# 11 of 16 down batches in seven products, W11 + W12 made in DRAM scratch, and activation forms three steps later, in a two-layer decoder trunk

## The chip, the cores and the metric

The kernel runs on one core of a Trainium2 chip. The metric is the device time of one execution in microseconds (us). The core's engines work side by side: TensorE multiplies, VectorE (DVE), ScalarE (ACT) and GpSimd (POOL) do the element-wise work, and SyncE (SP) issues the large DMAs. Each engine takes its instructions in a fixed order.

## The reference

Two decoder layers over 256 tokens of width 2048, all in float32: a token mixer (attention in layer 0, a gated recurrence in layer 1), then an MLP with a hidden width of 8192, then a gated per-layer embedding. The change is in the MLP; its end touches the embedding's input p.

```python
def sqrelu_mlp(xn, w_up, w_down):
    return jnp.square(jax.nn.relu(xn @ w_up)) @ w_down
...
        h = h + sqrelu_mlp(rmsnorm(h, g_mlp[i]), w_up[i], w_down[i])
        ple_gate = jax.nn.sigmoid(rmsnorm(h, g_ple[i]) @ w_ple_gate[i])
        h = h + ple_gate * (p[i] @ w_ple_proj[i])
```

## The kernel before

**Numbers in two parts.** A float32 operand is split into a high part (a cast, on ACT) and a low part (operand minus high part, on DVE), and a product is the sum of three products of parts. A unit of the weight stream, a *sub*, is 128 x 1024 weights. `stream` (L433) runs over all groups of subs: it has the weights loaded by SP in chunks of two to four subs (`load_to`), splits them three subs ahead of the matmuls (`split_to`, W_SPLIT - 1), and issues the matmuls. Raw chunks lie in a ring of four buffers in the MLP (three `w_raw`, one `big`), split pairs in a ring of six (four `w_hi`/`w_lo`, one pair `v4`, one `big`).

**The MLP.** The hidden width is cut into 16 batches of 512. `up(b)` (L820) makes the transposed hidden values of one batch, 8 subs with matmuls of 512 and 256 columns (L537). Its `evict` (L795) adds two halves (L804, L806), does relu and square on ACT (L807, L808) and splits the result. `down(half, bs)` (L826) multiplies the hidden values of some batches with one half of the columns of `w_down` and adds the product to the residual h. After each pair of up groups stands one down group: the first of batches 0 and 1, then of four batches each ({0..3}, {2..5}, ... {12..15}) with halves alternating, and at the end one more of {14, 15}. Per layer that is six groups of four batches that the change alters, batches up to 3, 5, 7, 9, 11 and 13.

**Seven products.** A down batch is a product of 2 x 2 blocks of the hidden values with 2 x 2 blocks of weights of 128 x 1024: W11 and W21 are the even and odd rows of 128 of the first chunk (512 columns), W12 and W22 those of the second. An even batch (`is_seven`) takes seven products of forms (`FORMS`) in place of eight: 7 subs of 6 matmuls = 42; an odd, plain one 4 subs of 12 = 48. For a seven the hidden side needs sums (L810, L814, L815), and the weight side four sums on DVE (L470): U1 = W11 + W12, T2 = U1 + W22, T3, T4. A form's high part is cast at L464, its low part is made at L471. Plain batches and up groups use L356 and L357. Sums, the evicted halves of a seven and kept products share three buffers of tag `t4`.

**After the products.** `middle` (L832) makes combinations of the products once the last of P1, P5, P6, P7 is there, and `evict` (L843) adds eight parts to h (L848).

**What sets the order.** The code issues a group's work in the order above, with `defer` for work that is to come some subs later; a scheduler then lays each engine's instructions in a row by what they depend on.

## Time and profile before

| | us |
|---|---|
| median of 3 runs | 2304.05 |
| lowest and highest run | 2304.01, 2304.63 |
| the profiled execution | 2303.79 |
| its span from first to last instruction | 2301.9 |
| TensorE busy in it | 2277.8 |
| DVE busy | 1709.6 |
| ACT busy | 1355.5 |

The page gives the busy time of each engine over the whole span. A table by stage gives the same for chosen stretches of time, a list of waits tells which engine waited for which, and a timeline shows single instructions: when one started, how long it took, and how long its engine had been idle before it and for whom. Consecutive instructions of an engine overlap a little, so the distance of their starts is less than their length.

### The profile page before, as it was taken

What the parts mean: (1) busy time and instruction counts of PE and PEld (TensorE: products, weight loads), DVE (VectorE), ACT (ScalarE), POOL (GpSimd) and SP (SyncE); (2) the same over time, 40 slices, a digit from 0 to 9 for tenths busy, and PEclk for the clock granted to TensorE, in tenths of its full rate; (3) what the DMA queues carried; (4) which work ended last, traced back from release to release, by engine and by line L of the source; (5) the groups of instructions that cost most, each with busy time, mean ns of one, the idle gap of its engine ahead of it and who ended that gap; (6) DMA issues with size and microseconds to landing.
All of it is one profiled execution on the core that took longest, in us unless ns stands there. A gap on an engine that the chain in (4) does not pass through costs nothing. (4 is left out here: it accounts for less than half of the span.)

```text
span 2301.9 us, 29004 instructions
## 1 busy us (share of the span) xinstructions
PE 2277.8 (99%) x11275; PEld 1913.4 (83%) x11275; DVE 1709.6 (74%) x2048; ACT 1355.5 (59%) x1836; POOL 47.3 (2%) x79
## 2 busy tenths in 40 slices
PE   8999999999999999999999999999999999999999
PEld 7888888888888888887888887888888888888787
DVE  6676655778878868879666767568887887887974
ACT  6555555655655645646557887555564564564653
POOL 2100000000000000000000000000000000000000
PEclk9999999999999999999999999999999999999999
DMA  7455556456547547545555565645745645745464
GB/s 244 165 185 168 165 171 214 168 182 237 181 162 242 187 161 244 175 162 186 193 190 190 165 201 173 202 157 200 256 151 179 238 167 181 239 167 179 174 210 146
DMA packets 221050, 434.80 MB, mean 189 GB/s; under 512 B 7326, under 2 KB 12064, under 8 KB 220912
## 3 DMA queue, kind: packets, MB, share of 16 engines
q1 hardware_dynamic: 220256, 432.04, 55.5%
q8 instruction: 88, 1.44, 0.3%
q0 software_dynamic: 608, 0.89, 0.2%
q14 instruction: 50, 0.41, 0.1%
q10 hardware_dynamic: 48, 0.02, 0.0%
HBM read 430.82 MB, written 2.10 MB: 188 GB/s over the span
## 5 line engine op out<-in xcount | busy, mean ns | idle before, releaser
L357 DVE TENSOR_TENSOR w_lo<-w_raw,w_hi 128x1024 fp32r<-128x1024 f32 x465 | 564.2, 1221 | 304.5 <-ACT w_hi L356 304.4
L356 ACT CAST w_hi<-w_raw 128x1024 fp32r<-128x1024 f32 x465 | 486.6, 1051 | 419.4 <-PE acc L352 214.9
L537 PE MATMUL acc<-x,w_hi 128*128 128x512 f32 x1368 | 477.3, 396 | 0.0
L350 PE MATMUL acc<-w_hi,x 128*128 128x512 f32 x1152 | 457.1, 397 | 0.0
L351 PE MATMUL acc<-w_lo,x 128*128 128x512 f32 x1152 | 450.4, 391 | 1.9 <-DVE w_lo L357 1.9
L352 PE MATMUL acc<-w_hi,x 128*128 128x512 f32 x1152 | 450.6, 391 | 0.0
L537 PE MATMUL acc<-x,w_lo 128*128 128x256 f32 x1368 | 368.5, 279 | 0.0
L537 PEld LDWEIGHTS acc<-x,w_hi 128*128 128x128 f32 x1368 | 251.9, 188 | 54.7
L537 PEld LDWEIGHTS acc<-x,w_lo 128*128 128x128 f32 x1368 | 257.8, 188 | 7.4
L352 PEld LDWEIGHTS acc<-w_hi,x 128*128 128x128 f32 x1152 | 216.7, 188 | 46.7 <-DVE x L357 0.2
L351 PEld LDWEIGHTS acc<-w_lo,x 128*128 128x128 f32 x1152 | 217.2, 189 | 44.9 <-DVE w_lo L357 3.1
L350 PEld LDWEIGHTS acc<-w_hi,x 128*128 128x128 f32 x1152 | 216.8, 188 | 41.7
L464 ACT CAST w_hi<-t 128x1024 fp32r<-128x1024 f32 x85 | 89.2, 1051 | 128.8 <-PE acc L537 73.9
L537 PE MATMUL acc<-x,big 128*128 128x512 f32 (+1 forms) x688 | 127.7, 338 | 0.0
L356 ACT CAST w_hi<-big 128x1024 fp32r<-128x1024 f32 x87 | 90.7, 1050 | 62.6 <-PE acc L537 26.7
L471 DVE TENSOR_TENSOR w_lo<-t,w_hi 128x1024 fp32r<-128x1024 f32 x85 | 103.8, 1222 | 30.3 <-ACT w_hi L464 30.1
L537 PE MATMUL acc<-x,v 128*128 128x512 f32 (+1 forms) x672 | 124.8, 338 | 0.0
L537 PEld LDWEIGHTS acc<-x,big 128*128 128x128 f32 x688 | 107.9, 188 | 15.5
L537 PEld LDWEIGHTS acc<-x,v 128*128 128x128 f32 x672 | 105.9, 188 | 15.0
L357 DVE TENSOR_TENSOR w_lo<-big,w_hi 128x1024 fp32r<-128x1024 f32 x87 | 105.3, 1218 | 14.1 <-ACT w_hi L356 14.1
L471 DVE TENSOR_TENSOR w_lo<-w_raw,w_hi 128x1024 fp32r<-128x1024 f32 x64 | 78.0, 1219 | 31.9 <-ACT w_hi L464 31.9
L518 PE MATMUL acc<-w_hi,x 128*128 128x512 f32 x256 | 100.3, 392 | 1.4 <-ACT w_hi L464 1.3
(277 smaller groups left out, 3570.0 us busy)
## 6 DMA issues: line engine op xcount, KB each, us to landing
w_raw<-in_w_up_dram SPq DMA_DIRECT2D x96, 1024.0 KB, 5.5
w_raw<-in_w_down_dram SPq DMA_DIRECT2D x96, 1024.0 KB, 5.2
w_raw<-in_w_qkv_dram SPq DMA_DIRECT2D x47, 1024.0 KB, 5.1
big<-in_w_up_dram SPq DMA_DIRECT2D x32, 1024.0 KB, 5.6
big<-in_w_down_dram SPq DMA_DIRECT2D x32, 1024.0 KB, 7.3
w_raw<-in_w_ple_gate_dram SPq DMA_DIRECT2D x32, 1024.0 KB, 5.2
w_raw<-in_w_in_rec_dram SPq DMA_DIRECT2D x32, 1024.0 KB, 5.4
w_raw<-in_w_o_attn_dram SPq DMA_DIRECT2D x16, 1024.0 KB, 5.1
```

The costliest lines, as they stand in the source:

```text
L350: nc.tensor.matmul(ps, lhsT=lh, rhs=rh, start=start, stop=False)
L351: nc.tensor.matmul(ps, lhsT=lh, rhs=rl, start=False, stop=False)
L352: nc.tensor.matmul(ps, lhsT=ll, rhs=rh, start=False, stop=stop)
L356: nc.scalar.copy(hi, src)
L357: nc.vector.tensor_tensor(lo, src, hi.bitcast(F32), op=ALU.subtract)
L464: nc.scalar.copy(s.hi, src)
L471: nc.vector.tensor_tensor(s.lo, src, s.hi.bitcast(F32), op=ALU.subtract)
L518: nc.tensor.matmul(acc[k], lhsT=lh, rhs=rh, start=first, stop=False)
L537: nc.tensor.matmul(o, lhsT=lh, rhs=rh, start=k == 0 and n == 0, stop=k == g.nk - 1 and n == 1)
```

## The change

Batches with b mod 4 = 0, 2 or 3, except 15, now go in seven products: 11 of 16. A down group of four batches has three sevens and one plain batch. U1 is no longer summed by DVE. For each seven GpSimd issues three DMAs into a DRAM buffer of a pool of ten: one element of h that the preceding down group wrote last, then W12's block, then W11's block with an accumulating write. They are issued at the second and the fourth sub of the first up group of the pair, and SP loads the result as half of the second chunk. T2, T3 and T4 stay DVE sums, in a changed order of forms. Relu, square, sums and splits of an evicted batch are deferred by three subs. Products are combined and added to h one by one as each is finished (`done`), the third seven of a group holds its hidden values in two `big` buffers, and one pair of the split ring lies in the space left in the `x32` tile (and `wx`). The setup of p moves to the end of its own layer's MLP.

```diff
--- before.py
+++ after.py
@@ -80,10 +80,10 @@
 FORMS = (
-    ("W11", X11, "P1"), ("U1", S1, "P5"), ("T2", S2, "P6"), ("T3", S3, "P7"), ("W21", X12, "P2"),
-    ("T4", X22, "P4"), ("W22", S4, "P3"),
+    ("W11", X11, "P1"), ("W21", X12, "P2"), ("W22", S4, "P3"), ("U1", S1, "P5"), ("T2", S2, "P6"),
+    ("T3", S3, "P7"), ("T4", X22, "P4"),
 )
-SUMS = {"U1": ("W11", "W12"), "T2": ("U1", "W22"), "T4": ("T2", "W21"), "T3": ("W12", "W22")}
+SUMS = {"T2": ("U1", "W22", ALU.add), "T3": ("T2", "W11", ALU.subtract), "T4": ("T2", "W21", ALU.add)}
 BT = 4
@@ -104,18 +104,34 @@
 class Blocks:
-    def __init__(self, w, b, n0):
+    def __init__(self, w, b, n0, seven):
         r0 = b * BT * P
         rows = w[r0 : r0 + BT * P].rearrange("(c p) n -> p c n", p=P)
-        self.chunks = [Chunk(rows[:, :, n0 + i * NB : n0 + (i + 1) * NB], BT) for i in range(2)]
-        for c in self.chunks:
+        cols = [rows[:, :, n0 + i * NB : n0 + (i + 1) * NB] for i in range(2)]
+        self.chunks = [Chunk(c, BT) for c in cols]
+        for i, c in enumerate(self.chunks):
             c.ring = 1
-        self.sums = {}
+            if seven:
+                half = lambda raw, i: raw[:, i * SK : (i + 1) * SK]
+                c.pieces = [(lambda raw, i=i: half(raw, i), cols[c is self.chunks[1]][:, i::2]) for i in range(2)]
+        self.sums, self.cols = {}, cols
+    def prepare(self, nc, scratch, after):
+        nc.gpsimd.dma_start(scratch[:1, 0, :1], after)
+        nc.gpsimd.dma_start(scratch, self.cols[1][:, 0::2])
+        dst, _ = self.chunks[1].pieces[0]
+        self.chunks[1].pieces[0] = (dst, scratch)
+        return lambda: nc.gpsimd.dma_start(scratch, self.cols[0][:, 0::2], accum_op=ALU.add)
     def of(self, name):
...
             return self.sums[name]
-        return self.chunks[int(name[2]) - 1].raw[:, int(name[1]) - 1 :: 2]
+        n, k = {"W11": (0, 0), "W21": (0, 1), "U1": (1, 0), "W22": (1, 1)}[name]
+        return self.chunks[n].raw[:, k * SK : (k + 1) * SK]
 class SevenGroup:
...
@@ -140,11 +157,11 @@
         self.first, self.last = {}, {}
+        self.aside = ("P4", "P7") if len(self.subs) % len(FORMS) else ("P4",)
         for i, (_, form, nj) in enumerate(self.what):
...
                 self.last[k] = i
-        self.mid = max(self.last[k] for k in ("P1", "P5", "P6", "P7"))
     @staticmethod
...
@@ -424,10 +442,10 @@
             return self.r[:, t : t + 1]
-        def feed(self, nb):
+        def feed(self, nb, after=1):
             self.stat(nb)
             for b in range(2):
-                defer(1 + b, lambda b=b: self.transpose(nb, b))
+                defer(after + b, lambda b=b: self.transpose(nb, b))
     def stream(groups):
...
@@ -481,9 +498,9 @@
                         s.hi, s.lo = (v4([P, SK, NB], F32R) for _ in range(2))
-                    elif at == 1:
-                        both = big([P, 2, SK, NB], F32R)
-                        s.hi, s.lo = both[:, 0], both[:, 1]
+                    elif at == 1 and "spare" in state:
+                        s.hi = state["spare"]
+                        s.lo = wk.tile([P, SK, NB], F32R, tag="wx", name="wx", bufs=1)
                     else:
@@ -513,14 +530,15 @@
                         if q[0] not in acc:
-                            acc[q[0]] = ps_tp.tile([P, NB], F32, name="tp") if q[0] in ("P3", "Z") else psum([P, NB])
+                            acc[q[0]] = ps_tp.tile([P, NB], F32, name="tp") if q[0] in g.aside else psum([P, NB])
                     for k, lh, ll, rh, rl, first, last in prods:
...
                         nc.tensor.matmul(acc[k], lhsT=lh, rhs=rl, start=False, stop=last)
-                    if i == g.mid:
-                        g.middle(acc)
+                    for k in acc:
+                        if g.last[k] == i:
+                            g.done(k, acc)
                 elif g.flip:
...
@@ -557,7 +577,8 @@
         nc.gpsimd.dma_start(p_sb, p[l, 0].rearrange("(t q) d -> q t d", q=P))
-        pT[l] = Operand(*(wk.tile([P, 2, SEQ], F32R, name="pT" + c, bufs=1) for c in "hl"))
+        both = big([P, 2, 2, SEQ], F32R)
+        pT[l] = Operand(both[:, 0], both[:, 1])
         def transpose():
@@ -771,22 +792,28 @@
     SLOTS = 4
+    ALONE = {"P2": (0, 0), "P4": (1, 0), "P3": (0, 1), "Z": (1, 1)}
     def is_seven(b):
-        return b % 2 == 0
+        return b % SLOTS != 1 and b != NBT - 1
     def mlp(l, norm_in, norm_out):
-        hid, space = {}, {}
+        hid, space, sums = {}, {}, []
         def batch(b):
+            at = b % SLOTS
             if not is_seven(b):
...
                 return Batch(False, both[:, 0], both[:, 1])
+            if at == 3:
+                return Batch(True, big([P, 2, 7, P], F32R), big([P, 2, 7, P], F32R))
             if "x" not in space:
-                space["x"] = x32([P, 2, 2, 2, 7, P])
-            both = space["x"][:, b % SLOTS // 2]
+                space["x"] = x32([P, 8, 2 * NB])
+                state["spare"] = space["x"][:, 7].rearrange("p (k n) -> p k n", k=SK)
+            both = space["x"].rearrange("p a n -> p (a n)")[:, : 28 * 2 * P]
+            both = both.rearrange("p (s h j f t) -> p s h j f t", s=2, h=2, j=2, f=7)[:, at // 2]
             return Batch(True, both[:, 0], both[:, 1])
...
@@ -804,6 +832,15 @@
                         nc.vector.tensor_tensor(halves[i], two(ps[:, :SEQ]), two(other), op=ALU.add)
+                    fs.append((j, f, x))
+                def finish():
+                    for e in fs:
+                        form(*e)
+                defer(3, finish)
+                def form(j, f, x):
                     nc.scalar.activation(x, x, AF.Relu)
@@ -827,38 +864,71 @@
             hs = [slice(n0 + i * NB, n0 + (i + 1) * NB) for i in range(2)]
-            keep = {}
...
+            keep, have = {}, set()
+            def add(t, n, part):
+                hb = h[:, t, hs[n]]
+                nc.vector.scalar_tensor_tensor(
+                    hb, in0=part, scalar=norm_in().r2[:, t : t + 1], in1=hb, op0=ALU.mult, op1=ALU.add
+                )
+            def done(k, acc):
+                have.add(k)
+                if k in ALONE:
+                    add(*ALONE[k], acc[k])
+                if k == "P1":
+                    c1 = t4([P, 2, NB])
+                    keep["P1"], keep["M"] = c1[:, 0], c1[:, 1]
+                    nc.scalar.copy(keep["P1"], acc["P1"])
+                if "A" not in have and {"P1", "P6"} <= have:
+                    have.add("A")
+                    nc.vector.tensor_tensor(keep["M"], keep["P1"], acc["P6"], op=ALU.subtract)
+                if "B" not in have and {"A", "P7"} <= have:
+                    have.add("B")
+                    cb = t4([P, 2, NB])
+                    keep["B"], keep["N"] = cb[:, 0], cb[:, 1]
+                    nc.vector.tensor_tensor(keep["B"], acc["P7"], keep["M"], op=ALU.add)
+                if "M" not in have and {"B", "P5"} <= have:
+                    have.add("M")
+                    for q, o in (("M", "M"), ("N", "B")):
+                        nc.vector.scalar_tensor_tensor(
+                            keep[q], in0=acc["P5"], scalar=-1.0, in1=keep[o], op0=ALU.mult, op1=ALU.subtract
+                        )
             def evict(acc):
...
+                for q, at in (("P1", (0, 0)), ("B", (1, 0)), ("M", (0, 1)), ("N", (1, 1))):
+                    add(*at, keep[q])
                 if bs[-1] == NBT - 1:
                     for n in range(2):
-                        norm_out().feed(2 * half + n)
...
         for b in range(0, NBT, 2):
+            at = len(groups)
             up(b)
...
             down(int(b % 4 == 0), range(max(b - 2, 0), b + 2))
-        down(1, range(NBT - 2, NBT))
+            if b == NBT - 2:
+                down(1, range(NBT - 2, NBT))
+            if b == NBT - 2:
+                groups[-1].closing = True
+            todo = [bl for g in groups[at + 2 :] for bl in g.sevens]
+            col = D // 2 * (1 + int(b % 4 != 0)) - 1
+            def copies(_, todo=todo, col=col):
+                for bl in todo:
+                    u1 = scratch.tile([P, SK, NB], F32, name="u1")
+                    sums.append(bl.prepare(nc, u1, h[:1, 1, col : col + 1]))
+            def adds(_):
+                while sums:
+                    sums.pop(0)()
+            groups[at].pre.update({1: copies, 3: adds})
     def ple(l, norm_in, norm_out):
```

How the order moves, at three places of the down group of batches 8 to 11 in layer 0. First DVE at the group's start. Here `acc` are the up group's products, `t1`, `t2` and `t4` the evicted values, `big` or `x32` a split's other part. Before, from the evict of batch 11 on:

```order
L806 TENSOR_TENSOR t2_7248<-acc_7070,t1_7249 128x2x128
L806 TENSOR_TENSOR t2_7248<-acc_7071,t1_7252 128x256
L806 TENSOR_TENSOR t2_7259<-acc_7072,t1_7260 128x2x128
L806 TENSOR_TENSOR t2_7259<-acc_7073,t1_7263 128x256
L471 TENSOR_TENSOR w_lo_7298<-t4_7287,w_hi_7297 128x1024
L357 TENSOR_TENSOR big_7247<-t2_7248,big_7247 128x512
L357 TENSOR_TENSOR big_7247<-t2_7259,big_7247 128x512
L471 TENSOR_TENSOR big_7272<-t4_7228,big_7272 128x1024
L471 TENSOR_TENSOR w_lo_7309<-w_raw_7182,w_hi_7308 128x1024
```

After, from the last weight split ahead of that evict:

```order
L488 TENSOR_TENSOR wx_7386<-w_raw_7325,x32_3628 128x1024
L834 TENSOR_TENSOR t4_7370<-acc_7181,t1_7371 128x2x128
L834 TENSOR_TENSOR t4_7370<-acc_7182,t1_7374 128x256
L834 TENSOR_TENSOR t4_7377<-acc_7183,t1_7378 128x2x128
L487 TENSOR_TENSOR t4_7388<-w_raw_7325 128x1024
L834 TENSOR_TENSOR t4_7377<-acc_7184,t1_7381 128x256
L847 TENSOR_TENSOR t4_7370<-t4_7370 128x256
L851 TENSOR_TENSOR t4_7370<-t4_7370 128x128
L852 TENSOR_TENSOR t4_7370<-t4_7370 128x128
L488 TENSOR_TENSOR w_lo_7399<-t4_7388,w_hi_7398 128x1024
L375 TENSOR_TENSOR big_7369<-t4_7370,big_7368 128x896
L847 TENSOR_TENSOR t4_7377<-t4_7377 128x256
```

The evicted batch is now a seven with sums of its own (L847, L851, L852), and the weight sums T2 (L487) and the low part behind it stand between its steps.

Second ACT at the same place. Before, from the casts of the copies on:

```order
L804 COPY t1_7263<-acc_7073 128x256
L464 CAST w_hi_7297<-t4_7287 128x1024
L807 ACTIVATE t2_7248<-t2_7248 128x512
L807 ACTIVATE t2_7259<-t2_7259 128x512
L808 ACTIVATE t2_7248<-t2_7248 128x512
L808 ACTIVATE t2_7259<-t2_7259 128x512
L356 CAST big_7247<-t2_7248 128x512
L356 CAST big_7247<-t2_7259 128x512
L464 CAST big_7272<-t4_7228 128x1024
L464 CAST w_hi_7308<-w_raw_7182 128x1024
```

After:

```order
L482 CAST w_hi_7305<-w_raw_7282 128x1024
L482 CAST w_hi_7328<-w_raw_7282 128x1024
L482 CAST v4_7348<-w_raw_7325 128x1024
L482 CAST x32_3628<-w_raw_7325 128x1024
L832 COPY t1_7371<-acc_7181 128x256
L832 COPY t1_7374<-acc_7182 128x256
L832 COPY t1_7378<-acc_7183 128x256
L844 ACTIVATE t4_7370<-t4_7370 128x512
L832 COPY t1_7381<-acc_7184 128x256
L845 ACTIVATE t4_7370<-t4_7370 128x512
L482 CAST w_hi_7398<-t4_7388 128x1024
```

Relu and square stood ahead of two casts of weights for the group's first subs; now four casts of the group's weights (L482) stand ahead of the copies.

Third TensorE at the end of that group, where `tp` are the last products. Before, from the last read of the low part `v4_7499` on:

```order
L521 MATMUL tp_7344<-v4_7499,big_7247 128x512 x2
L521 MATMUL tp_7395<-v4_7499,big_7247 128x512 x2
L518 MATMUL tp_7344<-big_7510,big_7247 128x512
L519 MATMUL tp_7344<-big_7510,big_7247 128x512
L518 MATMUL tp_7344<-big_7510,big_7247 128x512
L519 MATMUL tp_7344<-big_7510,big_7247 128x512
L518 MATMUL tp_7395<-big_7510,big_7247 128x512
L519 MATMUL tp_7395<-big_7510,big_7247 128x512
```

After:

```order
L535 MATMUL tp_7476<-w_hi_7679,big_7368 128x512
L536 MATMUL tp_7476<-w_hi_7679,big_7369 128x512
L535 MATMUL tp_7476<-w_hi_7679,big_7368 128x512
L536 MATMUL tp_7476<-w_hi_7679,big_7369 128x512
L555 MATMUL acc_7728<-x32_2934,w_hi_7689 128x512
L555 MATMUL acc_7729<-x32_2934,w_hi_7689 128x512
L555 MATMUL acc_7730<-x32_2934,w_hi_7689 128x512
L555 MATMUL acc_7731<-x32_2934,w_hi_7689 128x512
L538 MATMUL tp_7476<-w_lo_7680,big_7368 128x512 x2
L555 MATMUL acc_7728<-x32_2934,w_lo_7690 128x256 x2
```

The last low part of the group, `w_lo_7680`, is now read by the group's last two matmuls, and four matmuls of the next up group (L555) stand ahead of them. Where the DVE row of the low part `v4_7499` had 21 others of its size between it and the evict, `w_lo_7680` has 30.

## Rows read from the trace of the kernel before

**Rows 1.** The page: the span, and busy time, share and instructions by engine.

```profile
span 2301.9 us, 29004 instructions
...
PE 2277.8 (99%) x11275; PEld 1913.4 (83%) x11275; DVE 1709.6 (74%) x2048; ACT 1355.5 (59%) x1836; POOL 47.3 (2%) x79
```

**Rows 2.** Table by stage: four-batch groups with their sum, an up pair, last two groups.

```profile
core 0: us, PE busy (x) PEld busy (x) DVE busy (x) ACT busy (x) POOL busy (x), PEclk, DMA share, GB/s
513.66:554.68 41.02, 41.02 (x181) 33.77 (x180) 37.75 (x40) 27.97 (x32) 0.00 (x0) 1.00 0.76 260
599.57:642.31 42.74, 41.41 (x182) 33.69 (x180) 39.33 (x42) 28.10 (x32) 0.00 (x0) 1.00 0.73 249
...
sum 499.38, PE 494.06 PEld 404.93 DVE 458.31 ACT 329.85 POOL 0.00; mean PE 41.17 PEld 33.74 DVE 38.19 ACT 27.49 POOL 0.00
...
642.31:687.01 44.70, 44.70 (x257) 38.98 (x256) 30.50 (x37) 21.40 (x28) 0.00 (x0) 1.00 0.41 138
...
1032.50:1098.42 65.92, 64.19 (x288) 51.98 (x286) 60.88 (x70) 42.03 (x57) 0.00 (x0) 1.00 0.55 190
2131.17:2197.32 66.15, 64.52 (x287) 51.88 (x286) 61.65 (x71) 41.13 (x57) 0.00 (x0) 1.00 0.56 192
```

**Rows 3.** Waits of TensorE: for whom, us in total, times, longest.

```profile
PE acc L518 <- ACT big L464: 5.3, 4, 1.3
```

**Rows 4.** Timeline of ACT in the group from 599.57: start, us, what [idle before].

```profile
600.98 1.16 ACT L807 ACTIVATE t<-t 128x512 f32<-128x512 f32 x2
602.04 1.14 ACT L808 ACTIVATE t<-t 128x512 f32<-128x512 f32 x2
603.08 1.12 ACT L356 CAST big<-t 128x512 fp32r<-128x512 f32 x2
604.11 1.04 ACT L464 CAST big<-t 128x1024 fp32r<-128x1024 f32 x1
```

**Rows 5.** Timeline of TensorE, same place.

```profile
605.20 0.51 PE L518 MATMUL acc<-big,x 128*128 128x512 f32 x1 [1.33 <-ACT big L464]
```

**Rows 6.** Timeline of DVE, same group: first and last of 15 without a gap.

```profile
606.32 1.22 DVE L471 TENSOR_TENSOR w_lo<-w_raw,w_hi 128x1024 fp32r<-128x1024 f32 x1
...
622.37 1.22 DVE L471 TENSOR_TENSOR w_lo<-t,w_hi 128x1024 fp32r<-128x1024 f32 x1
```

**Rows 7.** Timeline of DVE where an evicted batch is a seven.

```profile
576.57 1.61 DVE L806 TENSOR_TENSOR t<-acc,t 128x256 f32<-128x256 f32 x4
...
580.39 0.75 DVE L810 TENSOR_TENSOR t<-t 128x256 f32<-128x256 f32 x2
581.06 0.48 DVE L814 TENSOR_TENSOR t<-t 128x128 f32<-128x128 f32 x2
581.47 0.48 DVE L815 TENSOR_TENSOR t<-t 128x128 f32<-128x128 f32 x2
581.87 1.22 DVE L357 TENSOR_TENSOR w_lo<-big,w_hi 128x1024 fp32r<-128x1024 f32 x1
583.00 2.08 DVE L357 TENSOR_TENSOR x<-t,x 128x896 fp32r<-128x896 f32 x2
```

**Rows 8.** Timeline of DVE towards the end of the group from 599.57.

```profile
626.34 0.68 DVE L836 TENSOR_TENSOR t<-t,acc 128x512 f32<-128x512 f32 x1
626.94 1.22 DVE L357 TENSOR_TENSOR w_lo<-w_raw,w_hi 128x1024 fp32r<-128x1024 f32 x1
...
631.01 1.21 DVE L357 TENSOR_TENSOR v<-big,v 128x1024 fp32r<-128x1024 f32 x1
...
642.57 1.40 DVE L848 SCALAR_TENSOR_TENSOR h<-tp,n_r,h 128x512 f32<-128x512 f32 x2
643.89 1.40 DVE L848 SCALAR_TENSOR_TENSOR h<-t,n_r,h 128x512 f32<-128x512 f32 x2
```

**Rows 9.** Timeline of TensorE at the same place.

```profile
638.63 1.09 PE L521 MATMUL tp<-v,big 128*128 128x512 f32 x4
```

**Rows 10.** DMA issues: out<-in, queue, count, KB each, median us to landing.

```profile
w_raw<-in_w_down_dram SPq DMA_DIRECT2D x96, 1024.0 KB, 5.2
...
big<-in_w_down_dram SPq DMA_DIRECT2D x32, 1024.0 KB, 7.3
...
w_raw<-in_w_ple_proj_dram SPq DMA_DIRECT2D x8, 512.0 KB, 3.7
...
t<-in_conv_b_dram POOLq DMA_DIRECT2D x1, 8.0 KB, 5.8
```

**Rows 11.** Timeline of SP's queue in the up pair from 642.31.

```profile
655.95 31.25 SPq L457 DMA_DIRECT2D w_raw<-in_w_down_dram  x4
```

43 lines of the change are left out of this document (15 added, 28 removed).

## The prediction, made before the changed kernel was run

> **What bounds the kernel now.** I read the page's busy shares first: TensorE is busy for 99% of the span, and DVE, the next, for 74% [rows 1]. Nearly all time is matmuls, so a change pays in the matmuls that it takes away, as long as nothing else begins to make TensorE wait. The table by stage comes second, because DVE's 74% is a mean. In the twelve down groups of four batches DVE is busy 458.31 of 499.38 us, 92%, and in an up pair 30.50 of 44.70 us [rows 2]. The down groups are where DVE has little left, and they are what the change shortens on TensorE. Third come the waits. Of the time that TensorE stands in the middle of the MLP, the largest piece is 5.3 us in four waits of 1.3 for a cast of ACT [rows 3]. They lie in four of the twelve down groups, which take 42.7 us against 41.0 to 41.1 of the other eight [rows 2]. In one of them ACT does the relu, square and casts of the up group that has just ended, and the cast that TensorE needs is queued behind these [rows 4]; the matmul behind it waited 1.33 us [rows 5].
>
> **What it removes on TensorE.** Twelve groups go from two seven-product batches and two plain ones to three and one: 3 x 42 + 48 = 174 matmuls for 2 x 42 + 2 x 48 = 180. That is 72 fewer. A step costs 41.02 / 180 = 0.228 us [rows 2]; **-16.4 us**. The other groups keep their counts.
>
> **The activation form three steps later.** In the four groups that wait, ACT's relu, square and casts now come behind casts that TensorE needs, or (where the last batch of the pair is a seven) behind four casts made ahead. 4 x 1.33 = **-5.3 us**. If something takes the place of that wait, it is DVE, and I count it there.
>
> **DVE in the down groups.** A seven costs DVE 11 operations of 128x1024 before (7 low parts, 4 sums) and 10 after, a plain batch 4. A group of four had 30 and now has 34, while its matmuls fall by 6. Back to back these operations start 16.05 us apart over 14 steps, 1.146 us each [rows 6].
>
> [...]
>
> The groups are now of two kinds. In kind A (batches up to 3, 7 or 11; six groups) the order is seven, plain, seven, seven, and the batch whose evict stands at the group's start is a seven. In kind B (up to 5, 9 or 13; six) it is seven, seven, seven, plain, behind a plain batch's evict.
>
> Kind A, laid out for the group that ends with batch 11 in layer 0. From the evict of that batch to the low part that the group's last two matmuls read, the new order has 31 operations of 128x1024 on DVE, 4 evict sums, 6 form sums, 2 splits of 128x896, 3 adds to h and one product sum. 31 x 1.146 = 35.5. The evict sums are 1.61 / 4 = 0.40 each, 1.6. The form sums, by the starts of their three pairs, 0.67 + 0.41 + 0.40 = 1.5. The splits 2.0 together (2.08 less the overlap) [rows 7]. The adds 0.66 each (1.32 for two by their starts) and the product sum 0.6 [rows 8]: 2.6. Together 43.2 us, beginning some 0.4 us before the up group ends, so the last low part comes at 42.8. TensorE wants it after 168 + 4 matmuls of the group and 4 of the next up group: 176 x 0.228 = 40.1. So at least 2.7 us of waiting even if DVE itself never waits. Before, the same stretch has 22 such operations, and the trace shows it: in the group that starts at 599.57 the last low part is done at 632.22 [rows 8] and first read at about 638.6 [rows 9], 6 us to spare. That cover is gone.
>
> I laid the order of the three kind A groups of a layer row by row at these steps. DVE alone gives waits of 4.5, 2.0 and 3.7 us (batch 3, 7, 11; they differ by what stands ahead of the last low part and by the first splits of the next up group). With ACT's casts and the buffers of split weights counted too it is 5.6, 3.0 and 4.2, since the three sums T2, T3, T4 of the first seven share three buffers with the two halves of the evicted batch. For two layers: 20.4 or 25.6. The same laying on the order of before gives a wait in just the four groups that have one, 0.86 for the measured 1.33, and none in the other eight, so I trust its place more than its size. I take **+22 us**, with ends of 12 and 32.
>
> Kind B by the same laying: the last low part of the third seven arrives at 31.3 us and is wanted at 31.4. 0 to 0.45 each, **+1 us**, ends 0 and 2.7.
>
> **The sum W11 + W12 in DRAM.** GpSimd issues for each seven a tiny DMA that waits for the last add to h of the preceding down group, a copy of 512 KB and an accumulating add of 512 KB. Behind the waiting one stand only the other DMAs of that kind. The adds to h end 3.0 us into an up pair (645.30 against 642.31) [rows 2, 8]. The trace has no DMA from DRAM to DRAM; the nearest rows are a tiny one from GpSimd, up to 5.8 us, a load of 512 KB, 3.7, and the slowest median for 1 MB, 7.3 [rows 10]. So the first sum stands 3.0 + 5.8 + 2 x (3.7 to 7.3) = 16 to 23 us into the pair. SP comes to a down group's first load 13.6 us into the pair (655.95) [rows 11], so it waits there up to some 9 us, with only later loads of the down group behind it; the load lands by about 31 of 44.7 us. If the three sevens of a group follow one another wholly, the third sum stands at 31 to 53 us and is wanted about 25 us into the down group, near 70. The traffic, 3 x 1 MB more for a group, lies in the up pair, where the DMA engines are at 41% [rows 2]. **0**, hidden under the up pair; if the cover went, every microsecond past its end would count twelve times.
>
> **The ends of the MLPs.** The transposes of p now stand at the very end of the last down group, with the first matmuls that read them right behind. TensorE then waits for a cast of 128x512, about 0.56 us (two in 1.12 [rows 4]), and its signal, and the low part comes behind adds to h (1.4 for two [rows 8]). 0.6 to 2.5 each; I take 1.0, **+2 us**. The last two groups of a layer stall 65.92 - 64.19 and 66.15 - 64.52, 3.4 us together [rows 2]; their sevens lose one DVE operation each (three to a layer, 3.4 us of DVE work), but the later form moves casts there. **-1 us**, ends -3.4 and +3.
>
> **Sum.** -16.4 - 5.3 + 22 + 1 + 0 + 2 - 1 = +2.3. The profiled execution took 2303.79 us (span 2301.9), the median of the runs 2304.05, 0.3 above; added to the median, **2306 us**. What TensorE no longer multiplies it spends waiting for DVE.
>
> **Rivals.**
> 1. DVE keeps up in kind A. For it: DVE is idle for 14.2 us of an up pair [rows 2], and the two layings differ by 5 us already. Against it: the order sets only four of the group's low parts ahead of the evict, so idle time in the up pair can't be used. With 0 to 10 us of kind A waits for 22 the time is 2284 to 2294. Chance 0.27.
> 2. Slower: the first seven of kind A gives its buffer of raw weights back only after T4, by the laying 11 to 13 us into the group, and the load of the second seven starts then. At 5.2 us [rows 10] it lands at 16 to 18, and DVE, by its order, asks for it at 16.6 to 18.5. That is the point from which it decides: a load of 7.3 us, or a T4 later by 2, makes DVE itself stand 2 to 3 us in each of the six groups, on top of the count. 2306 + 12 to 18, about 2321. Chance 0.18.
> 3. The scratch sum comes late, so that the change makes a wait of its own. It takes a first sum later than 44.7 - 7.3 = 37 us, each DMA step 14 us long; 5 us in twelve groups would be 2366. [...] Chance 0.03.
>
> **How the numbers follow.** The forecast has 0.52: its own ends are 2296 (kind A at 12) to 2317. Of it 0.38 lies within 0.2% of the time before (4.6 us, about what a measurement of this kernel can tell from no change), 2299.4 to 2308.7, 0.10 above, 0.04 below. With rival 1 faster has 0.31, with rivals 2 and 3 slower has 0.31. 8 in 10 reach from 2287 into rival 2, to 2319.
>
> **What would show it.** Kind A groups of 42 to 44 us with several waits of TensorE for DVE low parts, in the first 14 us and at the end; DVE busy for over 95% of them. Kind B groups of 39.7 to 40.2. No wait for an ACT cast at 5 us. SP waiting for the scratch sum some microseconds in the up pair, and TensorE never for that load. A wait of about 1 us for p at each MLP's end. I am wrong if kind A groups take 40 us (rival 1), or if DVE in them stands idle for a DMA (rival 2) or for U1 (rival 3).

## The result: 1.7% slower

The changed kernel takes 2343.54 us, the median of 4 runs (2342.53 to 2344.70), beside 2304.18 for the kernel before: a ratio of 1.0172, with a 95% interval of 1.0158 to 1.0186. The forecast was 2306 us. The profiled execution has a span of 2341.0 us.

The page of the changed kernel, the lines that answer to [rows 1]:

```profile
span 2341.0 us, 29305 instructions
...
PE 2282.3 (97%) x11203; PEld 1897.0 (81%) x11203; DVE 1766.4 (75%) x2124; ACT 1386.3 (59%) x1872; POOL 145.3 (6%) x211
```

TensorE issues 72 matmuls fewer and is busy for 4.5 us more. Its share of the span falls from 99 to 97%, so some 35 us of the loss are waits, and part of what remains of the matmuls ran slower.

The stages tell where. I grouped both traces by the starts of the matmuls; a stage ends where the next one's matmuls begin, in us for both layers together:

| stages | before | after |
|---|---|---|
| 16 up groups in pairs | 719.2 | 719.2 |
| 2 groups {0, 1} | 41.2 | 41.6 |
| 6 groups of kind A | 249.7 | 264.8 |
| 6 groups of kind B | 249.7 | 269.3 |
| last two groups of each layer | 132.1 | 136.5 |
| all else in the span | 910.0 | 909.6 |

Kind A was forecast at 6 x 39.7 + 22 = 260 us, kind B at 6 x 39.7 + 1 = 239. Kind A is near, 5 us over; kind B is 30 us off. The table by stage of the six kind B groups (columns as in [rows 2]):

```profile
602.75:647.04 44.29, 42.10 (x176) 33.54 (x175) 44.09 (x46) 29.57 (x36) 0.00 (x0) 0.96 0.70 239
780.76:825.88 45.12, 42.26 (x176) 33.57 (x175) 44.52 (x47) 30.27 (x38) 0.00 (x0) 0.96 0.70 237
...
2078.59:2122.24 43.65, 40.86 (x175) 32.27 (x174) 43.40 (x46) 29.01 (x34) 0.00 (x0) 1.00 0.71 242
sum 269.28, PE 249.74 PEld 195.81 DVE 266.83 ACT 180.78 POOL 0.00; mean PE 41.62 PEld 32.63 DVE 44.47 ACT 30.13 POOL 0.00
```

DVE is busy for 99% of them. The list of waits of the changed kernel has the two largest waits of TensorE in the MLP, the one of DVE for a transfer, and that of SP's queue for the scratch (whom, us in total, times, longest); the wait of [rows 3] for a cast on ACT in `big` is gone from it, and waits for other casts (L482) have come:

```profile
PE acc L535 <- DVE t L834: 13.8, 6, 3.0
PE tp L535 <- ACT w_hi L482: 6.4, 10, 1.0
...
DVE t L487 <- DMA w_raw<-in_w_down_dram: 72.4, 10, 10.2
...
SPq L475 <- DMA u<-in_w_down_dram: 135.1, 20, 11.1
```

TensorE waits six times, once in each kind B group, 13.8 us in all, for DVE's evict sums of the up group (L834). DVE waits ten times, up to 10.2 us, before T2 (L487), for a load of `w_down`: 8.6 to 10.2 us in the up pair ahead of each kind B group, and less at the two MLPs' ends. One kind B group shows how the two belong together. Its up pair begins at 735.25, its own matmuls at 780.76. The timeline of DVE (start, us, what, idle before):

```profile
759.86 1.23 DVE L375 TENSOR_TENSOR w_lo<-w_raw,w_hi 128x1024 fp32r<-128x1024 f32 x1 [0.45 <-ACT w_hi L374]
770.84 1.23 DVE L487 TENSOR_TENSOR t<-w_raw 128x1024 f32<-128x1024 f32 x1 [9.75 <-DMA w_raw<-in_w_down_dram]
771.98 0.75 DVE L847 TENSOR_TENSOR t<-t 128x256 f32<-128x256 f32 x2
...
784.55 1.21 DVE L488 TENSOR_TENSOR w_lo<-t,w_hi 128x1024 fp32r<-128x1024 f32 x1
785.69 1.41 DVE L834 TENSOR_TENSOR t<-acc,t 128x256 f32<-128x256 f32 x4
```

T2 = U1 + W22 stands in DVE's order in the middle of the up pair, ahead of the first evicted batch's form sums (L847). In kind A the first T2 stands behind the evict of the pair's last batch, 45 us after the pair's start, and waits for nothing. Here DVE comes to it at 761.1 and stands until 770.84. From there it works without a gap to the evict sums of the second up batch, at 785.69. Their products were there at 780.8. The third product of the group needs one of the buffers that hold them (of PSUM, where this kernel's matmuls write), so TensorE stands:

```profile
786.15 0.51 PE L535 MATMUL acc<-x 128*128 128x512 f32 x1 [2.44 <-DVE t L834]
...
787.32 0.63 PE L536 MATMUL acc<-x 128*128 128x512 f32 x1
...
788.60 0.63 PE L535 MATMUL acc<-w_hi,x 128*128 128x512 f32 x1
789.02 0.63 PE L536 MATMUL acc<-w_hi,x 128*128 128x512 f32 x1
```

After the wait a step takes up to 0.43 us (788.60 to 789.02, say) in place of 0.23, over nine matmuls: the granted clock is 0.83 from 780 to 790 us, and 0.50 from 787 to 789. In the six kind B groups I count 22.9 us of waits and 6.4 us of slower steps, against 3.0 and 0.2 before. About half of the 6.4 are steps of 0.38 to 0.43 in two of the groups, 602.75 and 780.76, whose granted clock is 0.96 where the other four have 1.00; the rest are mostly single steps of 0.33 to 0.34 behind a wait.

Why the load was late is seen in SP's queue and GpSimd's, in the same pair:

```profile
742.12 1.54 POOL L124 DMA_DIRECT2D u<-h  x3 [75.55 <-DVE h L871]
744.01 1.38 POOL L125 DMA_DIRECT2D u<-in_w_down_dram  x2 [0.35 <-DMA u<-h]
...
756.44 1.03 POOL L128 DMA_DIRECT2D u<-in_w_down_dram  x1 [2.69 <-DMA u<-in_w_down_dram]
```

```profile
749.80 0.88 SPq L475 DMA_DIRECT2D w_raw<-in_w_down_dram  x2
761.11 0.34 SPq L475 DMA_DIRECT2D w_raw<-u  x1
761.49 0.43 SPq L475 DMA_DIRECT2D w_raw<-in_w_down_dram  x1
```

SP comes to U1 at about 750.7 and waits until 761.11, 26 us into the pair. W22, the other half of that chunk, is behind it (761.49) and lands at about 770. And the table by stage of 5 us each shows what the DMA engines do meanwhile (the last two columns, their busy share and GB/s):

```profile
740.00:745.00 5.00, 3.87 (x22) 3.11 (x21) 5.00 (x6) 1.21 (x2) 2.53 (x5) 1.00 0.23 52
745.00:750.00 5.00, 5.00 (x31) 4.35 (x30) 4.77 (x5) 1.73 (x2) 1.04 (x2) 1.00 1.02 365
750.00:755.00 5.00, 5.00 (x30) 4.38 (x30) 2.45 (x2) 1.43 (x2) 2.11 (x2) 1.00 1.01 374
755.00:760.00 5.00, 5.00 (x31) 4.25 (x30) 2.69 (x6) 3.36 (x7) 1.03 (x1) 1.00 1.10 276
760.00:765.00 5.00, 5.00 (x31) 4.39 (x30) 1.09 (x1) 2.85 (x5) 0.00 (x0) 1.00 1.10 256
765.00:770.00 5.00, 5.00 (x30) 4.37 (x30) 0.00 (x0) 0.00 (x0) 0.00 (x0) 1.00 1.06 347
```

From 745 to 770 they are full (1.01 to 1.10): three copies, three accumulating adds and the next chunks' loads. So there were two candidates for the cause, SP's wait for the scratch and the full DMA engines, and a third, that DVE simply has too much to do in every group of three sevens.

### The profile page after: what moved, and what is told of

The parts are those of the page before. It is cut to its first block, busy times and chain, and to the rows that moved or that the text cites. A ratio compares the mean times of both kernels' runs of the same rounds, so it can differ in the third digit from the quotient of the medians.

```text
span 2341.0 us, 29305 instructions
## 1 busy us (share of the span) xinstructions
PE 2282.3 (97%) x11203; PEld 1897.0 (81%) x11203; DVE 1766.4 (75%) x2124; ACT 1386.3 (59%) x1872; POOL 145.3 (6%) x211
## 5 line engine op out<-in xcount | busy, mean ns | idle before, releaser
L375 DVE TENSOR_TENSOR w_lo<-w_raw,w_hi 128x1024 fp32r<-128x1024 f32 x452 | 548.3, 1221 | 284.9 <-ACT w_hi L374 284.5
L374 ACT CAST w_hi<-w_raw 128x1024 fp32r<-128x1024 f32 x452 | 470.4, 1050 | 368.0 <-PE acc L370 211.3
L555 PE MATMUL acc<-x,w_hi 128*128 128x512 f32 x1400 | 488.4, 396 | 3.0 <-ACT w_hi L374 2.3
L368 PE MATMUL acc<-w_hi,x 128*128 128x512 f32 x1152 | 457.3, 397 | 0.0
L370 PE MATMUL acc<-w_hi,x 128*128 128x512 f32 x1152 | 450.4, 391 | 0.0
L555 PE MATMUL acc<-x,w_lo 128*128 128x256 f32 x1400 | 377.2, 280 | 2.2 <-DVE w_lo L375 1.9
L555 PEld LDWEIGHTS acc<-x,w_hi 128*128 128x128 f32 x1400 | 258.1, 188 | 59.5 <-ACT w_hi L374 3.7
L555 PEld LDWEIGHTS acc<-x,w_lo 128*128 128x128 f32 x1400 | 263.5, 188 | 12.6 <-DVE w_lo L375 5.5
L488 DVE TENSOR_TENSOR w_lo<-w_raw,w_hi 128x1024 fp32r<-128x1024 f32 x100 | 119.4, 1217 | 25.0 <-ACT w_hi L482 25.0
L482 ACT CAST w_hi<-t 128x1024 fp32r<-128x1024 f32 x89 | 92.7, 1049 | 62.6 <-DVE t L487 48.6
L482 ACT CAST w_hi<-w_raw 128x1024 fp32r<-128x1024 f32 x100 | 102.3, 1049 | 43.6 <-PE acc L555 34.2
L555 PE MATMUL acc<-x,v 128*128 128x512 f32 (+1 forms) x672 | 125.1, 338 | 0.0
L555 PEld LDWEIGHTS acc<-x,v 128*128 128x128 f32 x672 | 106.0, 188 | 15.0
L555 PE MATMUL acc<-x,x 128*128 128x512 f32 x312 | 110.6, 396 | 1.3 <-DVE t L834 1.3
L487 DVE TENSOR_TENSOR t<-t,w_raw 128x1024 f32<-128x1024 f32 x88 | 106.8, 1216 | 0.2
L124 POOL DMA_DIRECT2D u<-h x44 | 22.9, 534 | 1183.9 <-DVE h L871 1021.9
L536 PE MATMUL acc<-w_hi,big 128*128 128x512 f32 x242 | 94.7, 391 | 0.0
```

The costliest lines, as they stand in the source:

```text
L368: nc.tensor.matmul(ps, lhsT=lh, rhs=rh, start=start, stop=False)
L370: nc.tensor.matmul(ps, lhsT=ll, rhs=rh, start=False, stop=stop)
L374: nc.scalar.copy(hi, src)
L375: nc.vector.tensor_tensor(lo, src, hi.bitcast(F32), op=ALU.subtract)
L482: nc.scalar.copy(s.hi, src)
L487: nc.vector.tensor_tensor(bl.sums[after], bl.of(one), bl.of(two), op=op)
```

## The experiments

Unless said otherwise a diff is against the changed kernel. The times of stages are made as in the table above.

**Copies without the wait.**

```diff
-        nc.gpsimd.dma_start(scratch[:1, 0, :1], after)
```

> The changed kernel without the tiny DMA that makes the scratch copies wait for the preceding down group's last add to h; the order of work on TensorE and ACT is the same, and on DVE nearly so. Theory L (the scratch sum is late: T2, which stands in DVE's order in the middle of the up pair, waits for the second chunk's load, DVE comes late to the evict sums, TensorE's third product of a kind B group waits for their PSUM buffer and its clock falls): the 9 to 10 us of DVE idle before T2 go, the waits of 22.9 us and most of the 6.4 us of slow steps in the six kind B groups go; 2343.5 - 26 = about 2317 us. Rival R (DVE has too little left in every group of three sevens, the scratch is hidden): kind B keeps its 44 to 45 us, 2341 to 2346 us.

2411.07 us, far off both. But the loss lies outside the MLPs. With nothing to hold them, GpSimd's copies and adds, each add waiting up to 12.1 us for its copy, stood ahead of its own small operations in the attention, and DVE waited for those:

```profile
PE tp L624 <- DVE t L611: 78.3, 5, 19.9
...
DVE t L611 <- POOL q_r L385: 85.4, 8, 20.7
```

In the MLPs kind B takes 239.8 us, as forecast, and kind A 265.1, as in the changed kernel. So kind B's loss comes with the scratch and not with three sevens, and the whole MLP part would be 4 us over the kernel before. DVE's wait before T2 falls from 72.4 us to 5.3, in six waits of up to 1.3. The run doesn't tell which of the two candidates it was, since both the wait and the copies' place went.

**U1 summed by DVE.**

```diff
+SUMS = {"U1": ("W11", "W12", ALU.add), "T2": ("U1", "W22", ALU.add), ...
...
-            groups[at].pre.update({1: copies, 3: adds})
```

> The changed kernel with U1 summed by DVE as before, without scratch (44 sums of 128x1024 more on DVE, at 1.146 us each). Theory L: no wait for a DMA, so kind B loses most of its 29 us of waits and slow steps but gets up to two sums in its tight stretch (0 to 14 us for six groups), kind A gets two or three in its own (14 to 20 us): 2330 to 2350 us. Rival R: the sums come on top of a DVE that is already the limit in all twelve groups, 12 x 3.4 us: 2375 to 2390 us.

2336.27 us (ratio 1.0143, 1.0126 to 1.0160): seven us faster than with the scratch. Kind B 247.0, kind A 287.2. Kind A takes 22 us more than in the changed kernel, 3.7 us a group; the three U1 sums of a group are three operations of 1.146 us, 3.4.

**The deferral alone**, in the kernel before: relu, square, sums and split of `up_evict` in a function that is deferred by three subs.

```diff
+                defer(3, finish)
```

> The kernel before with nothing but the activation form deferred by three subs. My term: the four waits of 1.3 us for a cast on ACT go, 2304.1 - 5.3 = about 2299 us. Rival: another wait takes their place, 2303 to 2306 us.

2297.64 us (0.9973, 0.9963 to 0.9983), 6.3 us faster than before. Kind A and kind B go from 249.7 to 246.5 us each: all twelve groups now take 41.0 to 41.1, and the four waits are gone.

**P3 in a spare PSUM buffer.**

```diff
-        self.aside = ("P4", "P7") if len(self.subs) % len(FORMS) else ("P4",)
+        self.aside = ("P4", "P3") if len(self.subs) % len(FORMS) else ("P4",)
```

> The changed kernel with the product P3 (the third of a group) in one of the two spare PSUM buffers in place of P7, so that the third product of a kind B group does not need a buffer of the up group. Theory L with the PSUM step: the wait 2.7 us into kind B groups goes or shrinks to under 1 us (the fourth product then asks 1.4 us later), with the slow steps behind it: 6 x 2 to 4 us less, 2320 to 2332 us. If DVE's lateness reaches TensorE through the low parts anyway, the wait only moves: 2338 to 2346 us.

2346.77 us (1.0189, 1.0174 to 1.0204), the case in which the wait only moves. The wait for L834 shrinks from 13.8 to 5.8 us, but kind B stays at 269.2: the wait moves to low parts and casts. So the PSUM buffer is only the first place at which DVE's lateness reaches TensorE.

**The wait a stage earlier.** The tiny DMA reads an element of the other half of h, which the down group before the preceding one wrote. TensorE, ACT and DVE have the same order row for row.

```diff
-            col = D // 2 * (1 + int(b % 4 != 0)) - 1
+            col = D // 2 * (1 + int(b % 4 == 0)) - 1
```

> The changed kernel with the tiny DMA reading an element of the other half of h, so that the scratch copies wait for the down group before the preceding one, a whole stage earlier; the order of work on TensorE, ACT and DVE is the same row for row. Theory L (the late scratch costs kind B its time, and the attention part of the run without any wait was slowed by GpSimd's early copies alone): kind B groups of 39.8 to 40.2 us, kind A as in the changed kernel, attention as before; the MLPs were 4 us over the kernel before in the run without a wait, so 2306 to 2311 us. Rival: the copies collide with other loads wherever they lie, 2330 us or more.

2341.22 us (1.0161, 1.0144 to 1.0178), 2.3 us less than the changed kernel, and kind B is at 269.4. What is won lies in the last two groups of each layer, 134.4 us for 136.5. The rival is right. The waits of SP and of DVE:

```profile
SPq L475 <- DMA u<-in_w_down_dram: 1.9, 2, 1.2
...
DVE t L487 <- DMA w_raw<-in_w_down_dram: 62.9, 8, 10.8
```

SP hardly waits for the scratch any more (1.9 us for 135.1), and DVE still waits 62.9 us for the load. SP now issues the two halves of the chunk 7 us sooner, U1 at 754.42 and W22 at 754.81, in a pair that begins at 735.31. They land at 769.0 and 771.0, no sooner than in the changed kernel, because they take 14.6 and 16.2 us (DMA issues from 754.2 to 755.2: KB each, us to landing):

```profile
w_raw<-u SPq DMA_DIRECT2D x1, 512.0 KB, 14.6
w_raw<-in_w_down_dram SPq DMA_DIRECT2D x1, 512.0 KB, 16.2
```

So taking away the wait of the queue is not enough. The copies, now those for the next group, still start 6 to 13 us into an up pair, and fill the DMA engines at the same time as before (busy share 0.99 to 1.10 from 745 to 770 us).

**Eight sevens, with the scratch late and early.**

```diff
-        return b % SLOTS != 1 and b != NBT - 1
+        return b % 2 == 0
```

> The changed kernel with the 8 even batches in seven products as before (252 matmuls more than... that is the count of the kernel before, 72 more than the changed kernel), scratch with its wait, deferral and the rest kept. Theory L: the scratch is as late as in the changed kernel, but DVE has one operation fewer for each seven and two plain batches to recover in; if lateness alone made the loss, groups behind a late sum still stand 1 to 4 us: 2305 to 2320 us. If it takes three sevens for a late sum to reach TensorE, nothing stands and the time is that of the deferral alone, 2296 to 2300 us.

> As the run before, with the scratch copies a stage earlier. Both theories: TensorE-bound, as the kernel before with the deferral alone, 2296 to 2300 us; any excess over that is what the other parts (product adds one by one, p at the end) cost.

2302.22 us (0.9993, 0.9984 to 1.0002) and 2302.01 us (0.9993, 0.9983 to 1.0002), no different from before, and 2 us above the 2296 to 2300 expected. Beside the deferral alone the second run is 4.4 us slower, about half of it in the last two groups (134.4 us for 132.1). In the first run kind A and kind B are at 247.8 each, without waits, although DVE waits 44.9 us in all for T2's load. But with two sevens in a group less is copied, and the load is up to 2.7 us late ahead of these twelve groups, against 8.6 to 10.2 ahead of kind B in the changed kernel. So DVE makes up for a load that is a little late; whether it could make up for 9 us with two sevens isn't shown.

**Without the sum T4**, on the run with the wait a stage earlier. T3 stands in T4's place, and that part of the product is left out.

```diff
+            if after == "T4":
+                bl.sums[after] = bl.sums["T3"]
```

> The run with the scratch copies a stage earlier, without the sum T4 (its place is taken by T3, so this part of the product is not computed): one DVE operation of 128x1024 fewer for each of the 44 sevens. If kind A groups are held by the count of DVE operations, as the prediction has it, each loses 2 to 3 x 1.146 us of its 3 to 5 us of waits: 13 to 20 us less than with T4, 2289 to 2296 us. If the chain of buffers or the loads hold them, under 5 us less.

2312.93 us, 28 us less, where 13 to 20 were expected. Kind A falls from 264.8 to 242.7 us, 3.7 us a group for three operations of 1.146, and comes to 40.1 us in four groups, where only matmuls are left. Without T4 buffers come free sooner too, but those did not hold DVE: in the six kind A groups of the changed kernel it is busy for 261.75 of 264.75 us. Kind A is held by the count of DVE's operations.

**The copies at another place of the pair.** The copies for a group are issued one pair earlier, and the tiny DMA reads an element of the first evicted batch's low part. The order on TensorE, ACT and DVE is again the same row for row.

```diff
...
+        for i in range(len(todos) - 1):
+            made = lambda b=2 * i: hid[b].lo[:1, 1, 0, :1].bitcast(F32)
+            groups[ats[i] + 1].pre.update({4: copies_of(todos[i + 1], made), 6: adds})
```

> The changed kernel with the scratch copies for a group issued one up pair earlier and at another point of the pair: the tiny DMA waits for an element of the low part of the first evicted batch, some 30 us into the pair, where SP has few loads in flight. The order of work on TensorE, ACT and DVE stays the same row for row. Theory C (not the wait for the scratch, but the DMA engines, which the copies and adds together with the next loads keep full from about 10 to 35 us into the up pair, bring the load that T2 reads 9 to 10 us late): kind B groups of 39.8 to 40.5 us, kind A unchanged, 2306 to 2312 us. Rival: the load is late for a reason that the copies' place does not touch (the ring of raw buffers, SP's order): kind B stays at 44 to 45 us, 2335 us or more.

2305.82 us (1.0009, 1.0000 to 1.0018). Nothing but the time at which the copies run has changed, and 37.7 us are back; 35.4 of them against the run with the wait a stage earlier. The sum of the six kind B groups, then DVE, the loads of U1 and W22 (issued at 750.54 and 750.93) and the DMA engines in the same pair, which begins at 731.46 here:

```profile
sum 239.53, PE 239.53 PEld 195.41 DVE 236.05 ACT 174.72 POOL 3.32; mean PE 39.92 PEld 32.57 DVE 39.34 ACT 29.12 POOL 0.55
```

```profile
756.63 1.23 DVE L487 TENSOR_TENSOR t<-w_raw 128x1024 f32<-128x1024 f32 x1
...
775.39 1.43 DVE L835 TENSOR_TENSOR t<-acc,t 128x256 f32<-128x256 f32 x4
```

```profile
w_raw<-u SPq DMA_DIRECT2D x1, 512.0 KB, 3.6
w_raw<-in_w_down_dram SPq DMA_DIRECT2D x1, 512.0 KB, 5.6
```

```profile
750.00:755.00 5.00, 5.00 (x31) 4.39 (x30) 3.06 (x6) 3.05 (x6) 0.00 (x0) 1.00 0.94 322
755.00:760.00 5.00, 5.00 (x31) 4.39 (x30) 4.59 (x9) 4.14 (x7) 0.00 (x0) 1.00 0.67 225
760.00:765.00 5.00, 5.00 (x31) 4.37 (x30) 5.00 (x6) 3.45 (x5) 1.95 (x4) 1.00 0.22 78
```

T2 runs at 756.63 and waits for nothing, the evict sums run at 775.39, before the up group ends, and kind B groups take 39.9 us, all of it TensorE. The loads that T2 needs have the DMA engines to themselves and land by 756.5; GpSimd's tiny DMAs begin at 762.78 and the copies at 764.60, 33 us into the pair for 6 to 13. Loads that SP issues beside the copies are as slow as before (four from 768 to 773 take 7 to 13 us), but nothing asks for them in time to wait.

So the sharing of the DMA engines is enough to make the loss, as the run before with the wait a stage earlier shows, and without it and SP's wait there is none. A run with SP's wait and free DMA engines was not made. In the changed kernel SP issues W22 25 to 27 us into a kind B pair, behind that wait; with the 5.1 to 6.5 us that the load takes here it would land 30 to 33 us in, so by this estimate the wait alone would be late for T2 as well.

**T2 in DRAM too**, for the three sevens of each kind A group: a copy and two accumulating adds more for each, and a load by SP into T2's buffer.

> The run with the copies at the other point of the pair, with T2 = W11 + W12 + W22 of the three sevens of each kind A group made in DRAM scratch as well (a copy and two accumulating adds more, and a load of 512 KB by SP into T2's own buffer): one DVE operation of 128x1024 fewer for 18 of the 44 sevens, all in kind A. By the count of DVE operations kind A loses 3.4 us a group, some 20 us in all: 2284 to 2293 us, faster than both kernels. If the DMA engines become the bound, or SP's queue stands behind the load of T2: 2305 us or more.

2380.74 us (1.0339, 1.0321 to 1.0356), the slow case. DVE has less to do and TensorE waits more: kind A 296.7, kind B 268.5, where none of the sums changed place. DVE waits 23.7 us for T2's loads. SP's queue or the DMA engines as the reason were not told apart.

**The deferral undone**, in the changed kernel and in the one with the copies moved.

```diff
-                defer(3, finish)
+                finish()
```

> The changed kernel with the activation form made at once in the evict, as before. My term for the deferral was 5.3 us in all, in the four groups where a cast was queued behind it; in the changed kernel every group now has three sevens, so if the same queue forms 5 us into all twelve groups it is up to 12 x 1.3 = 16 us: 2344 to 2360 us. If DVE's lateness hides it, 2340 to 2344 us.

> The run with the copies at the other point of the pair (2305.8 us), with the activation form made at once in the evict. My term for the deferral, 1.3 us where a cast is queued behind relu and square, should show now that no late load hides it: 5 to 16 us more, 2311 to 2322 us. If DVE, not ACT, is last at every group's start, no difference: 2304 to 2308 us.

2344.72 us (1.0177, 1.0162 to 1.0192), no different from the changed kernel. Its stages move by up to 5.5 us either way (kind A 270.2, last two groups 142.0, up pairs 714.2), so it isn't shown that DVE's lateness hides the deferral there. With the copies moved it is 2378.54 us (1.0323, 1.0307 to 1.0338), far above both expectations; DVE waits 31.3 us for T2's load into a `big` buffer, and SP 91.0 us for a load of its own. In one pair the two halves of that chunk are issued 42 us in, for 12 and 20 us with the deferral. Undoing the deferral moved loads as well, so this run doesn't measure ACT's queue, and what the deferral is worth there stays open.

**Splits further ahead**, on the run with the copies moved: in the MLP four and then five subs ahead of the matmuls in place of three. The form for five:

```diff
-                split_to(j + W_SPLIT - 1)
+                n = j + W_SPLIT - 1
+                while n + 1 < min(j + W_SPLIT + 2, len(subs)) and all(q.chunk.ring for q in subs[j : n + 2]):
+                    n += 1
+                split_to(n)
```

> The run with the copies at the other point of the pair, and in the MLP the splits issued four subs ahead of the matmuls in place of three. In the order of DVE this moves T2 and its low part of the first seven of a kind A group ahead of the evict: 29 operations of 128x1024 for 31 in the stretch that the prediction laid out. If the count in that stretch holds kind A, it loses up to 2 x 1.146 us a group: 2292 to 2299 us. If the ring of split buffers keeps DVE from running ahead, 2303 to 2307 us.

> As the run before with five subs ahead, which fills the ring of six pairs. By the count one or two operations fewer again in the kind A stretch: 2287 to 2296 us. If the ring is full already, as with four: the same time within 2 us; if DVE then works on far subs before near ones, slower than with four.

2295.49 us (0.9964, 0.9950 to 0.9978), as expected, and 2284.08 us (0.9916, 0.9901 to 0.9930), 3 us below its range. The second is 0.8% faster than the kernel before, and 13.6 us faster than the deferral alone. In the group that the prediction laid out, the stretch from the evict to the last low part has 27 operations of 128x1024 in its order for 31, since T2, T3 and two low parts now stand ahead of the evict. The six kind A groups, then the six of kind B:

```profile
sum 243.32, PE 241.98 PEld 195.97 DVE 232.24 ACT 170.14 POOL 1.92; mean PE 40.33 PEld 32.66 DVE 38.71 ACT 28.36 POOL 0.32
```

```profile
sum 239.53, PE 239.53 PEld 195.56 DVE 238.62 ACT 174.53 POOL 11.98; mean PE 39.92 PEld 32.59 DVE 39.77 ACT 29.09 POOL 2.00
```

With four subs ahead (29 operations) kind A and the up pairs lose 6 us together, where the count would give up to 14, and the rest of the gain lies in the last two groups of the layers (134.4 to 130.6). The other 8 us of kind A are seen in DVE's idle time there, 11.6 us for 2.9 with three subs ahead; its largest wait is one for ACT's square ahead of the form sums, 5.4 us in six groups. No run takes that wait away.

**Adds to h at the group's end.**

```diff
-                if k in ALONE:
-                    add(*ALONE[k], acc[k])
...
-        self.aside = ("P4", "P7") if len(self.subs) % len(FORMS) else ("P4",)
+        self.aside = ("P2", "P3") if len(self.subs) % len(FORMS) else ("P4",)
```

> The run with the copies at the other point of the pair, with all eight adds to h at the group's end as in the kernel before (P2 and P3 in the spare PSUM buffers): in DVE's order one add fewer (0.66 us) ahead of the last low part of a kind A group. By the count 0.7 us a group, 2300 to 2304 us; if the next up group then waits for the PSUM buffers, 2306 us or more.

2321.77 us (1.0081, 1.0066 to 1.0096). Kind A with the up pairs is as before this edit (981.7 for 979.7). The last two groups of each layer take 145.5 us for 134.4, where transposes now wait for adds to h and for the spare PSUM buffers. That cost was in neither expectation.

## Why the prediction was wrong, step by step

**The scratch term failed: 0, hidden; it cost 37.7 us**, the difference between the changed kernel and the one with the copies moved. In the profiled executions it is 36.2, of that 29.8 us kind B's, 4.2 the up pairs', 2.1 the last two groups'. The step has three parts. First, the deadline. I put it at the end of the up pair, 44.7 us in, and named 37 us as the point from which a late sum decides. That is right for kind A, where T2 stands 45 us in. But ahead of kind B DVE's order asks for T2 about 25 us into the pair, ahead of the form sums of the first evicted batch and so ahead of all that follows on DVE. So the 31 us at which I let the load land was already 6 us too late there, by my own numbers. Second, the load. I let the mean of 41% for the pair stand for its first half [rows 2]. The DMA engines are full from 10 to 35 us into the pair. There a copy of 512 KB takes 7.2 us in the median, within my 3.7 to 7.3, but an add takes 11.0, and W22's load 7.3 to 10.4 for the 3.7 of [rows 10]; it lands 33 to 36 us in. Third, SP's wait, which I did see and priced at up to 9 us (it is up to 11.1). Taken away by itself it gives back 2 us, in the last two groups, and nothing in kind B.

The traces show how much the DMA engines are shared: in the changed kernel they are 101 to 110% busy from 745 to 770 us, and a load of 512 KB (`w_raw` from `u`) that lands in 3.6 us with the copies moved takes 14.6 beside the copies and adds, in the run with the wait a stage earlier. How GpSimd issues them doesn't show as a cause: in the changed kernel an issue of a copy or add on GpSimd takes 0.65 to 1.12 us, and of its 131.7 us of idle time ahead of these, 127.0 are put down to a DMA before it.

**Rival 3, the late scratch, was the case that came**, at a chance of 0.03. Its condition, a first sum later than 37 us, did not come: the sum of the pair shown stands at 761.0, 26 us in, near my 16 to 23. The point was wrong, the full DMA engines are missing from it, and its 5 us fell in six groups, not twelve. I gave it so little because I had put the first read in a kind B pair some 20 us too late.

**Kind B, +1, failed for that reason.** 269.3 us measured for 239 forecast; with the copies moved it is 239.5. My laying counted on T2 being made in time.

**Kind A, +22, was right.** With the copies moved, kind A is 15.0 us over before and the up pairs 4.2 under, 10.8 together, where the forecast had 22 less six matmuls in six groups (8.2) less its two waits (2.7), 11.1. That DVE's count is the reason is shown by the run without T4, the one with U1 on DVE, and the one with five subs ahead. That rival 2, a late raw buffer, did not come is shown by DVE's idle time, 3 us in all six groups, none of it for a DMA. The place was not quite right: I named waits for low parts, and inside the groups TensorE waits for casts on ACT, 10.3 us in 14 waits. Nearly all of these casts had waited for a weight sum on DVE, so DVE's count reaches TensorE one step earlier, as here at the end of the group from 691.76, where T4's sum ran on DVE until 731.58:

```profile
731.61 1.04 ACT L482 CAST v<-t 128x1024 fp32r<-128x1024 f32 x1 [1.08 <-DVE t L487]
732.71 0.50 PE L535 MATMUL tp<-v,big 128*128 128x512 f32 x1 [1.19 <-ACT v L482]
```

**The step of DVE.** With the copies moved the starts of DVE's operations of 128x1024 stand 1.13 to 1.14 us apart (four steps from 762.40 to 766.94): the step measured before, 1.146, holds.

**The matmuls, -16.4**, hold: where nothing else waits, kind B takes 239.5 us for 246.5, 7.0 us less, beside 36 x 0.228 = 8.2.

**The deferral, -5.3**, measured -6.3 alone.

**The ends of the MLPs, +2 and -1.** With the copies moved the last two groups are 2.3 us over before, for +1. The wait for p is there at the end of each MLP, 0.7 us for the 1.0 that I took; the rest was not measured apart.

**Together**: without the scratch's cost the sum of the prediction, 2306, is the time that was measured, 2305.8. This is not luck of one total: the parts stand near their terms too, +10.8 for +11.1 in kind A with the up pairs, -10.2 for -10.5 in kind B, +2.3 for +1 at the ends. The range missed because the one term set to zero was the one whose cover lay in time, not in the mean.

## What to carry to other kernels

Whether a transfer was hidden hung here on how busy the DMA engines were when it ran (a load of 512 KB took 3.6 us with the copies moved, 14.6 beside them) and on where its first reader stood in its own engine's order (T2 45 us into the pair ahead of kind A, about 25 ahead of kind B): look up both the row that reads it, in every kind of stage, and the busy share of those microseconds, not the mean of the stage. When an engine has spare time in one stage and none in the next, let its work run further ahead before cutting operations: five subs ahead gave 22 us, and made the change worth having. A wait that is taken away and moves nothing was not the only cause: look what comes last behind it, here the load itself. An experiment that keeps the compute order row for row and moves only the transfers can tell.

## What the runs showed of the hardware

In the changed kernel accumulating adds in DRAM took about twice as much of the DMA engines' time as copies did for the same bytes. GpSimd's queue (software) has copies alone in flight from 745 to 750 us and adds alone from 760 to 765; SP's queue (hardware) has loads in both (packets, MB, share of the 16 engines):

```profile
q1 hardware_dynamic: 490, 0.97, 56.0%
q0 software_dynamic: 256, 0.86, 46.3%
...
q0 software_dynamic: 353, 0.69, 74.3%
q1 hardware_dynamic: 304, 0.59, 35.7%
```

That is 54% of these 5 us for a MB of copies, 108% for a MB of adds, and 58 and 61% for a MB of loads.

GpSimd's DMAs and its own small operations stood in one line in the run without the wait: the early copies and adds held the operations of the attention back, and DVE waited 85.4 us for those, up to 20.7 at a time.

In the changed kernel a wait of 2.4 us on TensorE was followed by nine steps of 0.35 to 0.43 us (786.15 to 789.88), at a granted clock of 0.50 from 787 to 789 us: 1.7 us on top of the wait. The other of the two kind B groups in which this came had steps of 0.38 to 0.43 from 609.16 to 612.52, at a clock of 0.57 from 609 to 613 us, behind a wait of 1.9. In the other four, behind waits of 1.3 to 3.0 us, the steps were back at 0.23 after one of 0.33 or 0.34, and the clock was 1.00.
